# Differential attention: coefficients once per head, scores one step ahead of their maxima, combination and products later

## The chip, the cores and the metric

The kernel runs on one core of one Trainium2 chip. The metric is the device time of one execution in microseconds (us). TensorE is called PE below (its weight loads PEld), VectorE DVE, ScalarE ACT, GpSimd POOL, and SyncE, which issues most of the weight loads from memory, SP.

## What is computed

One inference step of a four-layer trunk on 384 tokens: 128 context tokens and 256 latent ones. The layers mix tokens by differential attention, windowed attention, axial attention and a recurrent scan, in this order, and each is followed by a gated feed-forward. The change is in layer 0, the differential attention: each of 8 heads has two score maps, and the output uses the difference of their softmaxes.

```python
def block(qb, _):
    s = jnp.einsum('bqhmd,bkhmd->bhmqk', qb, keys) * (HEAD_DIM ** -0.5)
    p = jax.nn.softmax(s, axis=-1)
    a = p[:, :, 0] - lam * p[:, :, 1]
    return jnp.einsum('bhqk,bkhe->bqhe', a, vals)
```

Latent queries see 128 cached context keys and 256 latent keys (384 columns); context queries see 128 keys. After the block the head's output is normalised and goes through the output matrix.

## The kernel before

**Layout.** Weights stream in 512 KB units (SP), are split into a rounded and a remainder part (ACT `w_hi`, DVE `w_lo`), and each product is done three times over these parts (`mm3`, lines 394 to 397). Beside this, rows of the conditioning matrices ("ada" units, 512 KB each, issued by POOL into three buffers) are turned into modulation columns. Such a unit has one of two forms (`ada_parts`, line 311): on PE it is a `product` of 16 small matmuls (L336), an ACT copy `row` (L339), and a `turn` of two matmuls (L345) with a DVE copy (L346); on DVE it is two long multiply-reduce instructions (`reduce`, L327).

**Layer 0's attention** (`attn_layer`, line 762) is 24 items `i = (c, t)`: 8 heads `c`, and for each head the query chunks `t` in the order 1, 2, 0, two with 384 keys and then the one with 128. The work of an item is cut into functions: `scores` (two maps on PE, one PSUM bank each, lines 962 to 980), `maxima` (DVE, one per map), `exps` (ACT, one per map, each with its row sum), `inverse` and `coefficient` (DVE, one column each), `combine` (DVE, first map plus coefficient times second), `turn_p` (PE transposes, ACT copy), `pv` (PE products with the values). At a head's end come `finish` (ACT squares), `finish_2` (a chain of small DVE and ACT steps and one DVE multiply), and `turn_o` (PE transposes, ACT `oh` and DVE `ol`, L1107 to L1115).

**Order.** A list of events (lines 1134 to 1166) places every function in a step by a number and within the step by a rank: `at(e, rank, f)`. `advance()` plays one step in order of rank. Step 0 is played inside the last projection slice, steps 1 to 24 in a loop (line 1252) in which PE and DVE run exactly in the written order. ACT and SP run in written order in the whole kernel. So each engine's queue is this list, and an instruction that waits holds back all that stands behind it on its engine. The steps that are left after 24 are handed to `w_o` (line 653), the output matrix, which plays one or more after each of its first rounds `k`. There the planner may interleave PE's and DVE's instructions.

In step `e` the list before is: scores of item e (rank 0); an ada unit in some steps (`fill`, rank 0.5 in the steps with e mod 6 = 0, 1, 4; at rank 1.6 for e mod 6 = 2, 5; here the units of steps 0, 1, 4 mod 6 are in the PE form, the others one DVE reduce each); inverse of item e-1 (1.0); first maximum of item e (1.1); coefficient of e-1 (1.2); second maximum of e (1.3); combine of e-1 (1.5); exps of e (3); turn_p of e-2 (4); turn_o of an earlier head (4.5); pv of e-3 (5); `fill_end`, the turn of the ada unit (5.5); finish of a head (6).

**Buffers.** Scores use four PSUM banks in rotation (`banks(s=(0, 1, 2, 4), ...)`, line 1186), two per item, so the scores of item e take the banks of item e-2 and need its maxima and exps done. The same ring gives the first four blocks of `w_o` their banks. Transposes, ada products and ada turns share two banks (`tr`). The probabilities `p` have seven buffers, the statistics `ast` three.

Of the kernel before, what the change touches and what calls it, by code (L numbers as in the profile page):

```python
# [9 lines left out]
F32 = mybir.dt.float32  # L10
# [3 lines left out]
ALU = mybir.AluOpType  # L14
# [5 lines left out]
TOK = 384  # L20
# [35 lines left out]
RS = (0,1,2,4)  # L56
N7 = 4
PREP = 3
RK = (1.0, 1.1, 1.2, 1.3, 1.5, 2.5, 5.5)
DBANKS = dict(acc=(4, 5, 1, 2, 3), tr=(7, 0, 6))  # L60
RMS_AT = 1
ATT_A = (2, 3, 1, 1, 2, 1, 0)
ATT_B = (3, 4, 2, 1, 1, 3, 0)
LN_EXP = "natural_log_exp_and_others"
SILU = "silu_and_others"
# [83 lines left out]
def trunk(ctx: ExitStack, tc: tile.TileContext, a):  # L149
    nc = tc.nc  # L150
    V, S, G, T = nc.vector, nc.scalar, nc.gpsimd, nc.tensor
# [5 lines left out]
    sm = ctx.enter_context(tc.tile_pool(name="sm", bufs=4))  # L157
# [19 lines left out]
    def work(n=TOK):  # L177
        return wk.tile([128, n], F32, name="w", tag="w")
# [36 lines left out]
    st = dict(dma=0, split=0, blk=0, col=0, raw={}, hi={}, lo={}, look=3)  # L215
# [546 lines left out]
    def attn_layer(li, att, nd):  # L762
        diff = li == 0
# [8 lines left out]
        if diff:  # L772
            lamv = att.tile([128, 4, 64], F32, name="lamv", tag="lamv")
            lam = att.tile([128, 4], F32, name="lam", tag="lam")
            neglam = lam[:, 3:4]
# [174 lines left out]
        events, state, out, last = {}, {}, {}, [None]  # L950

        def at(e, rank, f, *args):
            events.setdefault(e, []).append((rank, len(events.get(e, [])), f, args))
# [2 lines left out]

        def stats_of(c):
            if ("st", c) not in state:
                state["st", c] = sm.tile([128, 8, 6], F32, name="ast", tag="ast", bufs=3)
            return state["st", c]  # L960

        def scores(i, c, t):
# [19 lines left out]
        def maxima(m, i, c, t):  # L982
            j, ps = 2 * t + m, state["s", i][m]
            V.tensor_reduce(out=stats_of(c)[:, 0, j:j + 1], in_=ps, op=ALU.max, axis=AX.X, negate=True)  # L984

        def exps(i, c, t):
            st_ = stats_of(c)
            state["p", i] = []
            for m, ps in enumerate(state.pop(("s", i))):
                j = 2 * t + m  # L990
                w = ps.shape[1]
                p = att.tile([128, TOK + 1], F32, name="p", tag="p")
                S.activation(out=p[:, :w], in_=ps, func=AF.Exp, bias=st_[:, 0, j:j + 1], accum_out=st_[:, 1, j:j + 1])  # L993
                state["p", i].append(p[:, :w - (li == 1)])

        def inverse(i, c, t):
            j = slice(2 * t + int(diff), 2 * t + 2)
            V.reciprocal(out=stats_of(c)[:, 2, j], in_=stats_of(c)[:, 1, j])

        def coefficient(i, c, t):  # L1000
            st_ = stats_of(c)
            V.scalar_tensor_tensor(out=st_[:, 2, 2 * t:2 * t + 1], in0=st_[:, 1, 2 * t:2 * t + 1], scalar=neglam,
                                   in1=st_[:, 2, 2 * t + 1:2 * t + 2], op0=ALU.mult, op1=ALU.mult)

        def combine(i, c, t):

# [127 lines left out]
        n_items = len(items)  # L1134
        tl, pl, cl, man, pend_at, n0, r0 = ATT_A if diff else ATT_B
        for i, (c, t) in enumerate(items):
            args = (i, c, t)
            at(i, 0, scores, *args)
            if diff:
                at(i + 1, RK[0], inverse, *args)  # L1140
                at(i, RK[1], maxima, 0, *args)
                at(i + 1, RK[2], coefficient, *args)
                at(i, RK[3], maxima, 1, *args)
                at(i + 1, RK[4], combine, *args)
                at(i, 3, exps, *args)
                for rank, what in ADA_A[i % len(ADA_A)]:
                    at(i, rank, fill, what)
                at(i + int(RK[6] < 0), abs(RK[6]), fill_end)
            else:
                at(i + 1, 1, maxima, 0, *args)  # L1150
                at(i + 1, 1.1, maxima, 1, *args)
                at(i + 1, 3, exps, *args)
                at(i + cl, 3.1, inverse, *args)
                for m in range(2):
                    at(i + cl, 3.2, divide, m, *args)
            at(i + tl, r0 + 4, turn_p, *args)
            at(i + pl, r0 + 5, pv, *args)
            if i % 3 == 2:
                at(i + pl, r0 + 6, finish, c)
                if not diff:  # L1160
                    at(i + pl + 1, 3.3, finish_low, c)
                if diff:
                    f = i + pl
                    for step_, (e, r) in enumerate(FIN):
                        at(f + e, r, finish_2, step_, c)
                    at(f + FIN[-1][0] + 1, r0 + 4.5, turn_o, c)
        place = [0]

        def advance():
            e = place[0]  # L1170
            place[0] += 1
            for _, _, f, args in sorted(events.pop(e, []), key=lambda x: x[:2]):
                f(*args)
            return e
# [76 lines left out]
        with tc.manual_schedule(engines={mybir.EngineType.PE, mybir.EngineType.DVE}) if man else nullcontext():  # L1251
            while place[0] < n_items + 1:
                i = advance()
# [292 lines left out]
    def body():  # L1546
        nd = None
        for li in range(4):
            ad["limit"] = (LIM0, 144, 184, 184)[li]
            if li == 3:  # L1550
                while ad["done"] < ad["load"]:
                    ada_step()
                ada_ctx.close()
            with ExitStack() as es:
                pool = es.enter_context(tc.tile_pool(name=f"mix{li}", bufs=1))
                nd = attn_layer(li, Att(pool), nd) if li < 3 else hgrn_layer(li, pool, nd)
            banks(acc=(2, 3, 4, 5, 0, 1) if li < 3 else (5, 1, 0, 2, 3, 4), tr=(6, 7))
            ad["limit"] = min((li + 2) * 48 - LIMF, ad["load"]) if li < 3 else 192
            st["look"] = LOOKF[li]
            with ExitStack() as es:  # L1560
                if li == 3:
                    more_ada(es.enter_context(tc.tile_pool(name="ada3", bufs=1)))
                nd = ffn(li, nd, es.enter_context(tc.tile_pool(name=f"ffn{li}", bufs=1)))

    class Att:
        BUFS = dict(xh=3, p=7)

        def __init__(self, pool):
            self.pool = pool
# [1 line left out]
        def tile(self, shape, dt, name, tag, bufs=None):  # L1571
            return self.pool.tile(shape, dt, name=name, tag=tag, bufs=bufs or self.BUFS.get(tag, 1))

# [118 lines left out]
```

## Time and profile before

| what | value |
|---|---|
| median of 3 runs | 1898.87 us (1896.47 to 1899.49) |
| the profiled execution, its own time | 1898.86 us |
| its span in the profile | 1897.1 us |
| granted PE clock, mean | 0.996 of full speed |
| busy share of the span | PE 99%, DVE 80%, ACT 47%, POOL 6% |
| attention steps of layer 0 | from about 125 us to about 187 us of the span |

The span is what the profiler saw of the program; the execution's own time is 1.8 us longer. A busy share says how long an engine had an instruction in work, not that the instruction was needed then. In a row of the timeline the first number is the start from the span's start, the second the time taken, then engine, line, operation, output and inputs; in brackets stands how long the engine had been idle before, and what it had waited for. [...]

### The profile page before, as it was taken

Reading aid. Unit: us, or ns where it says so; the run is one execution under the profiler, and the core shown is the slowest. Engines: PE = TensorE matmul, PEld = TensorE weight load, DVE = VectorE, ACT = ScalarE, POOL = GpSimd, SP = SyncE. Lnnn points to the kernel's source line nnn. Section 1 sums busy time; section 2 is a strip of 40 time slices with the busy share of each in tenths; the row PEclk is TensorE's granted clock in tenths of the full one; section 3 lists DMA queues with packets and bytes.
Section 4 is the critical chain, followed back from the end, with each engine's and each line's share of the span. In section 5 each row is a group of like instructions: output and inputs, shape, how many; then the busy total and the mean of one; then the engine's idle time right before and its main releaser. Section 6 shows DMA issues by size and latency. Waiting matters only on the chain.

```text
span 1897.1 us, 29939 instructions
## 1 busy us (share of the span) xinstructions
PE 1871.4 (99%) x11200; PEld 1744.5 (92%) x11200; DVE 1523.2 (80%) x3012; ACT 896.2 (47%) x1754; POOL 109.1 (6%) x207
## 2 busy tenths in 40 slices
PE   9998999999999999999999999999999999999999
PEld 6876999999975999999975999999989989999999
DVE  6999899995788999994688999994758897964442
ACT  6458553234467553234467553234456665632331
POOL 0011001110000001110000001110000000000000
PEclk9999999999999999999999999999999999999999
DMA  9664568775330558774330568774433324554442
GB/s 373 221 190 140 156 195 264 253 260 161 111 117 1 175 186 263 255 258 141 109 117 1 172 187 265 253 240 132 122 112 113 110 89 140 169 166 129 121 127 67
DMA packets 90741, 315.93 MB, mean 167 GB/s; under 512 B 10976, under 2 KB 14944, under 8 KB 90340
## 3 DMA queue, kind: packets, MB, share of 16 engines
q1 hardware_dynamic: 63508, 217.86, 36.0%
q0 software_dynamic: 26656, 95.97, 16.3%
q8 instruction: 88, 1.44, 0.3%
q14 instruction: 57, 0.47, 0.1%
q10 hardware_dynamic: 432, 0.20, 0.0%
HBM read 309.78 MB, written 4.20 MB: 166 GB/s over the span
## 4 chain that ended last, share of the span: by engine, by line
PE 91%; DVE 5%; ACT 3%; DMA 1%; issue 0%; ACTq 0%; DVEq 0%; SPq 0%
PE b L395 24%; PE b L397 24%; PE b L396 24%; PE b L628 3%; PE b L629 3%; PE b L632 3%; PE b L514 2%; PE b L970 1%; ACT p L993 1%; PE b L1064 1%; PE b L1040 1%; DVE ast L984 1%; PE b L911 1%; DMA ada<-in_ada_dram 0%; DVE junk L327 0%
## 5 line engine op out<-in xcount | busy, mean ns | idle before, releaser
L243 DVE TENSOR_TENSOR wl<-raw,wh 128x1024 fp32r<-128x1024 f32 x384 | 467.2, 1221 | 156.0 <-ACT wh L233 155.5
L233 ACT CAST wh<-raw 128x1024 fp32r<-128x1024 f32 x384 | 399.1, 1047 | 352.5 <-PE b L396 198.0
L397 PE MATMUL b<-fhh,wl 128*128 128x384 f32 x1280 | 433.9, 339 | 0.0
L396 PE MATMUL b<-fhl,wh 128*128 128x384 f32 x1280 | 432.4, 338 | 0.0
L395 PE MATMUL b<-fhh,wh 128*128 128x384 f32 x1280 | 432.4, 338 | 0.0
L327 DVE CUSTOM_DVE_ANT_0 junk<-ada,condb 128x1024 bf16<-128x1024 f32 x312 | 380.1, 1218 | 2.2
L397 PEld LDWEIGHTS b<-fhh,wl 128*128 128x128 f32 x1280 | 241.8, 189 | 0.0
L396 PEld LDWEIGHTS b<-fhl,wh 128*128 128x128 f32 x1280 | 241.8, 189 | 0.0
L395 PEld LDWEIGHTS b<-fhh,wh 128*128 128x128 f32 x1280 | 241.5, 189 | 0.0
L395 PE MATMUL b<-fh,wh 128*128 128x384 f32 x704 | 239.0, 339 | 0.0
L397 PE MATMUL b<-fh,wl 128*128 128x384 f32 x704 | 237.4, 337 | 0.0
L396 PE MATMUL b<-fl,wh 128*128 128x384 f32 x704 | 237.4, 337 | 0.0
L699 ACT CAST fh<-w 128x384 fp32r<-128x384 f32 x88 | 45.2, 514 | 288.2 <-DVE w L705 280.2
L395 PE MATMUL b<-xh,wh 128*128 128x386 f32 (+1 forms) x448 | 155.1, 346 | 0.0
L397 PE MATMUL b<-xh,wl 128*128 128x386 f32 (+1 forms) x448 | 152.6, 341 | 0.0
L396 PE MATMUL b<-xl,wh 128*128 128x386 f32 (+1 forms) x448 | 151.5, 338 | 0.0
L298 POOL DMA_DIRECT2D ada<-in_ada_dram x176 | 93.3, 530 | 986.8 <-DVE mod L327 771.4
L397 PEld LDWEIGHTS b<-fh,wl 128*128 128x128 f32 x704 | 132.3, 188 | 0.0
L396 PEld LDWEIGHTS b<-fl,wh 128*128 128x128 f32 x704 | 132.2, 188 | 0.0
L395 PEld LDWEIGHTS b<-fh,wh 128*128 128x128 f32 x704 | 132.1, 188 | 0.0
L412 DVE SCALAR_TENSOR_TENSOR x<-b,mod,x 128x128 f32<-128x128 f32 x192 | 69.6, 411 | 40.0 <-PE b L397 39.8
L705 DVE TENSOR_TENSOR w<-b,w 128x384 f32<-128x384 f32 x80 | 44.4, 555 | 58.8 <-PE b L397 58.6
(263 smaller groups left out, 2856.0 us busy)
## 6 DMA issues: line engine op xcount, KB each, us to landing
raw<-in_w_dram SPq DMA_DIRECT2D x384, 512.0 KB, 4.3
ada<-in_ada_dram POOLq DMA_DIRECT2D x176, 512.0 KB, 4.6
a0s<-in_ada_dram SPq DMA_DIRECT2D x8, 512.0 KB, 9.6
ada<-in_ada_dram SPq DMA_DIRECT2D x8, 512.0 KB, 9.6
x<-in_x_dram SPq DMA_DIRECT2D x4, 384.0 KB, 5.3
out_y_dram<-x SPq DMA_DIRECT2D x8, 192.0 KB, 1.9
condb<-saved SPq DMA_DIRECT2D x1, 1024.0 KB, 11.7
s<-in_state_dram POOLq DMA_DIRECT2D x8, 128.0 KB, 2.4
```

What stands on the lines that cost most here:

```text
L233: S.copy(out=hi, in_=st["raw"][u])
L243: V.tensor_tensor(out=lo, in0=st["raw"].pop(u), in1=st["hi"][u].bitcast(F32), op=ALU.subtract)
L298: (nc.gpsimd if i >= 16 else nc.sync).dma_start(out=t, in_=a["ada"][i])
L327: V.tensor_tensor_reduce(out=ad["junk"], in0=raw, in1=ad["cond"][:, j, :], op0=ALU.mult, op1=ALU.add, scale=1.0, scalar=0.0, accum_out=out ...
L395: T.matmul(out=out, lhsT=lh, rhs=rh, start=start, stop=False)
L396: T.matmul(out=out, lhsT=lh, rhs=rl, start=False, stop=False)
L397: T.matmul(out=out, lhsT=ll, rhs=rh, start=False, stop=stop)
L412: V.scalar_tensor_tensor(out=x[:, d, c0:c1], in0=ps[:, c0:c1], scalar=gate[:, d, j:j + 1], in1=x[:, d, c0:c1], op0=ALU.mult, op1=ALU.add)
L628: T.matmul(out=ps[t], lhsT=hh[:, k, c], rhs=wh, start=k == 0, stop=False)
L629: T.matmul(out=ps[t], lhsT=hh[:, k, c], rhs=wl, start=False, stop=False)
L632: T.matmul(out=ps[t], lhsT=hl[:, k, c], rhs=wh, start=False, stop=k == KC - 1)
L699: S.copy(out=fh[:, j, :], in_=m)
```

## The change

It moves the places in the list. The scores of item e stay in step e, and its maxima and exps come in step e+1. The two column operations that were done for each item (`inverse`, `coefficient`) are done once for a head over three columns (`coefficients`, at rank 1.0 in the step after the head's last exps). Combine comes four steps after the item's scores (`cl`, before one), `turn_p` five (before two), `pv` six (before three). The turn of an ada unit (`fill_end`) moves from rank 5.5 of its own step to rank 0.4 of the next one, behind that step's scores. To hold more items in flight, the statistics get five buffers, the first map's probabilities six, and the second map's go into the ring of five work tiles. `inverse` itself remains for the other layers.

```diff
--- before.py
+++ after.py
@@ -56,10 +56,10 @@
 RS = (0,1,2,4)
 N7 = 4
 PREP = 3
-RK = (1.0, 1.1, 1.2, 1.3, 1.5, 2.5, 5.5)
+RK = (1.0, 1.1, 1.2, 1.3, 1.5, 2.5, -0.4)
 DBANKS = dict(acc=(4, 5, 1, 2, 3), tr=(7, 0, 6))
 RMS_AT = 1
-ATT_A = (2, 3, 1, 1, 2, 1, 0)
+ATT_A = (5, 6, 4, 1, 2, 1, 0)
 ATT_B = (3, 4, 2, 1, 1, 3, 0)
 LN_EXP = "natural_log_exp_and_others"
 SILU = "silu_and_others"
@@ -956,7 +956,7 @@
 
         def stats_of(c):
             if ("st", c) not in state:
-                state["st", c] = sm.tile([128, 8, 6], F32, name="ast", tag="ast", bufs=3)
+                state["st", c] = att.tile([128, 8, 6], F32, name="ast", tag="ast", bufs=5 if diff else 3)
             return state["st", c]
 
         def scores(i, c, t):
@@ -989,18 +989,20 @@
             for m, ps in enumerate(state.pop(("s", i))):
                 j = 2 * t + m
                 w = ps.shape[1]
-                p = att.tile([128, TOK + 1], F32, name="p", tag="p")
+                p = work(TOK) if diff and m else att.tile([128, TOK + 1], F32, name="p", tag="p", bufs=6 if diff else 7)
                 S.activation(out=p[:, :w], in_=ps, func=AF.Exp, bias=st_[:, 0, j:j + 1], accum_out=st_[:, 1, j:j + 1])
                 state["p", i].append(p[:, :w - (li == 1)])
 
         def inverse(i, c, t):
-            j = slice(2 * t + int(diff), 2 * t + 2)
+            j = slice(2 * t, 2 * t + 2)
             V.reciprocal(out=stats_of(c)[:, 2, j], in_=stats_of(c)[:, 1, j])
 
-        def coefficient(i, c, t):
+        def coefficients(c):
+
             st_ = stats_of(c)
-            V.scalar_tensor_tensor(out=st_[:, 2, 2 * t:2 * t + 1], in0=st_[:, 1, 2 * t:2 * t + 1], scalar=neglam,
-                                   in1=st_[:, 2, 2 * t + 1:2 * t + 2], op0=ALU.mult, op1=ALU.mult)
+            V.reciprocal(out=st_[:, 2, 1:6:2], in_=st_[:, 1, 1:6:2])
+            V.scalar_tensor_tensor(out=st_[:, 2, 0:6:2], in0=st_[:, 1, 0:6:2], scalar=neglam,
+                                   in1=st_[:, 2, 1:6:2], op0=ALU.mult, op1=ALU.mult)
 
         def combine(i, c, t):
 
@@ -1137,12 +1139,12 @@
             args = (i, c, t)
             at(i, 0, scores, *args)
             if diff:
-                at(i + 1, RK[0], inverse, *args)
-                at(i, RK[1], maxima, 0, *args)
-                at(i + 1, RK[2], coefficient, *args)
-                at(i, RK[3], maxima, 1, *args)
-                at(i + 1, RK[4], combine, *args)
-                at(i, 3, exps, *args)
+                at(i + 1, RK[1], maxima, 0, *args)
+                if i % 3 == 2:
+                    at(i + 2, 1.0, coefficients, c)
+                at(i + 1, RK[3], maxima, 1, *args)
+                at(i + cl, RK[4], combine, *args)
+                at(i + 1, 3, exps, *args)
                 for rank, what in ADA_A[i % len(ADA_A)]:
                     at(i, rank, fill, what)
                 at(i + int(RK[6] < 0), abs(RK[6]), fill_end)
@@ -1563,7 +1565,7 @@
                 nd = ffn(li, nd, es.enter_context(tc.tile_pool(name=f"ffn{li}", bufs=1)))
 
     class Att:
-        BUFS = dict(xh=3, p=7)
+        BUFS = dict(xh=3)
 
         def __init__(self, pool):
             self.pool = pool
```

## Rows read from the trace of the kernel before

**Rows 1.** Busy time of each engine in stretches: the attention loop, the output matrix

```profile
core 0: us, PE busy (x) PEld busy (x) DVE busy (x) ACT busy (x) POOL busy (x), PEclk, DMA share, GB/s
...
140.00:155.00 15.00, 13.05 (x128) 9.35 (x129) 13.87 (x52) 12.60 (x54) 2.39 (x5) 1.00 0.43 142
...
200.00:212.00 12.00, 12.00 (x69) 11.49 (x68) 10.27 (x25) 6.35 (x15) 0.00 (x0) 1.00 0.42 132
```

**Rows 2.** Waits between 125 and 194 us: engine, line, releaser, total us, times, longest

```profile
DVE ast L998 <- ACT p L993: 2.9, 9, 0.5
...
ACT p L993 <- DVE ast L984: 8.6, 17, 1.3
```

**Rows 3.** Timeline of DVE, 161 to 168 us, steps 13 to 16

```profile
161.65 0.56 DVE L984 TENSOR_REDUCE ast<-b 128x1 f32<-128x384 f32 x1 [0.25 <-PE b L970]
...
163.93 0.15 DVE L346 COPY mod<-b 128x2 f32<-128x2 f32 x1
...
164.18 0.27 DVE L984 TENSOR_REDUCE ast<-b 128x1 f32<-128x128 f32 x1
...
164.70 0.61 DVE L1008 SCALAR_TENSOR_TENSOR p<-p,ast 128x384 f32<-128x384 f32 x1
165.23 1.22 DVE L327 CUSTOM_DVE_ANT_0 junk<-ada,condb 128x1024 bf16<-128x1024 f32 x1
...
166.37 0.61 DVE L1114 SCALAR_TENSOR_TENSOR ol<-b,subg,oh 128x384 fp32r<-128x384 f32 x1
166.90 0.15 DVE L998 RECIPROCAL ast<-ast 128x1 f32<-128x1 f32 x1
166.97 0.54 DVE L984 TENSOR_REDUCE ast<-b 128x1 f32<-128x384 f32 x1
167.43 0.21 DVE L1002 SCALAR_TENSOR_TENSOR ast<-ast,lam 128x1 f32<-128x1 f32 x1
```

**Rows 4.** Timeline of PE, 160 to 164 us, steps 13 and 14

```profile
160.70 0.92 PE L970 MATMUL b<-kT,qT 64*128 64x384 f32 x4
161.96 0.64 PE L336 MATMUL b<-ada,condP 128*32 128x128 f32 x16 [0.34 <-ACT pt L1023]
...
163.37 0.28 PE L345 MATMUL b<-quarter,row 128*128 128x2 f32 x2
163.58 0.49 PE L970 MATMUL b<-kT,qT 64*128 64x128 f32 x4
```

**Rows 5.** Timeline of ACT, 159 to 175 us, steps 12 to 18

```profile
159.94 0.58 ACT L993 ACTIVATE p<-b,ast 128x384 f32<-128x384 f32 x1 [0.87 <-DVE ast L984]
...
161.01 0.19 ACT L993 ACTIVATION_READ_ACCUMULATOR p<-b,ast 128x1 f32 x1
...
162.83 0.59 ACT L993 ACTIVATE p<-b,ast 128x384 f32<-128x384 f32 x1
...
171.62 0.37 ACT L993 ACTIVATE p<-b,ast 128x128 f32<-128x128 f32 x1 [0.56 <-DVE ast L984]
...
172.23 0.20 ACT L993 ACTIVATION_READ_ACCUMULATOR p<-b,ast 128x1 f32 x1
...
172.69 0.60 ACT L1113 ACTIVATE oh<-b,subg 128x384 fp32r<-128x384 f32 x1
...
174.68 0.58 ACT L993 ACTIVATE p<-b,ast 128x384 f32<-128x384 f32 x1 [0.46 <-DVE ast L984]
```

**Rows 6.** Timeline of all engines: exps of items 1 and 22, first w_o product

```profile
135.22 0.21 ACT L993 ACTIVATION_READ_ACCUMULATOR p<-b,ast 128x1 f32 x1
...
185.45 0.19 ACT L993 ACTIVATION_READ_ACCUMULATOR p<-b,ast 128x1 f32 x1
...
185.77 0.44 PE L395 MATMUL b<-oh,wh 128*128 128x384 f32 x1
```

**Rows 7.** Chain of waits near the loop's end: start, us, what

```profile
184.63 0.67 PE b L1052 x6
...
186.56 0.33 PE b L1021 x3
```

## The prediction

> **What bounds the kernel now.** I read the windows first, to see what the changed stage is short of. In the attention loop DVE is busy 13.87 of 15 us, PE 13.05, ACT 12.60; in the output matrix after it PE is busy the whole time [rows 1]. So a microsecond of PE work costs its full price behind the loop and little inside it, where DVE is nearly full. Then the waits: over the loop DVE loses only 2.9 us, to the exps that its reciprocal needs, and ACT loses 8.6 us, waiting for a maximum [rows 2]. Then the timeline, for the pace. From the exps of step 12 to those of step 18 it takes 174.68 - 159.94 = 14.74 us for six steps, two heads [rows 5].
>
> The round that sets this pace is: exps end, DVE's reciprocal, first maximum, next exps. DVE fills the gaps with combine, reduces and the heads' ends. PE is ahead of this round: the scores of step e need the banks of item e-2, whose exps ended a step earlier.
>
> **The prices.** A pair of exps takes 161.01 + 0.19 - 159.94 = 1.26 us with 384 keys, and 172.23 + 0.20 - 171.62 = 0.81 with 128 [rows 5]. A first maximum takes 0.54 (128 keys: 0.27), and the next DVE instruction starts 0.46 behind its start; combine 0.53, reduce 1.14 and the head's `ol` 0.53 from start to start [rows 3]. Both score maps take 0.92 (128 keys: 0.49), a turn 0.28 [rows 4]. That the first maximum waits for both maps is seen in its start at 161.65, 0.95 after the scores' [rows 3, 4]. From a product's start to the exps behind its row copy it is 162.83 - 161.96 = 0.87 [rows 4, 5]. From a 128-key pair's end to the end of `oh` it is 172.69 + 0.60 - 172.43 = 0.86 [rows 5].
>
> **Part by part.** *Coefficients once per head.* Of 24 reciprocals and 24 coefficients 8 each are left. The next instruction starts 0.07 behind a reciprocal, and a coefficient takes at most its 0.21 [rows 3]; 32 fewer give 16 × 0.07 + 16 × 0.21 = 4.5 us at most. DVE also no longer waits for each exps, up to the 2.9 us [rows 2]. This counts only where DVE sets the end.
>
> *Scores one step ahead.* Now the exps of item e-2 run in step e-1, so the scores of step e, the first thing on PE in that step, wait for the exps just ended. Everything behind them on PE waits too: the turn, the product, transposes and pv. The four banks are the limit, and the change adds none.
>
> *The turn moved behind the scores.* Its DVE copy is now the first DVE instruction of the step, ahead of coefficients, maxima and combine. In steps 1, 2 and 5 of six a turn is pending, so DVE stands until exps end, scores, turn, copy (0.15 [rows 3]), and only then forms the maximum that the next exps need. From exps end to exps end:
> - Steps 2 and 5 (the new scores are 128 keys): 0.49 + 0.28 + 0.15 + 0.54 + 1.26 = 2.72.
> - Step 1 (384 keys, coefficients first, reciprocal 0.15 and coefficient 0.21 in sequence): 0.92 + 0.28 + 0.15 + 0.36 + 0.54 + 1.26 = 3.51.
> - Step 4 has no turn but a product, whose ACT copy stands ahead of the exps: 0.92 + 0.87 + 1.26 = 3.05.
> - Steps 2 and 3 together go by DVE: copy ends at 0.92, two maxima 0.92, combine 0.53, reduce 1.14, which is 3.51. `ol` waits for `oh` until 2.72 + 0.86 = 3.58; with it 4.11, the 128-key maximum 0.27, the pair 0.81: 5.19.
> - Steps 5 and 0 together: the product's path is longer, 2.72 + 0.92 + 0.87 + 0.81 = 5.32.
>
> Six steps are 3.51 + 5.19 + 3.05 + 5.32 = 17.07 us, against 14.74.
>
> *Start and end of the loop.* Before, the exps of item 1 end at 135.43 and those of item 22 at 185.64, 21 steps in 50.21 us [rows 6]. After, item 0's exps fall in step 1, at about the place of item 1's (taken as equal), and item 22's in step 23, 22 steps later: three sixes, 51.21, and steps 20 to 23, 2.72 + 2.47 + 3.05 + 2.72 = 10.96. The first steps lack work: step 2 has no combine and no `ol` yet (1.13 less for steps 2 and 3), step 8 no `ol` (0.6 less). That makes 60.4 us, 10.2 more. The first product of the output matrix takes the bank of item 22's first map and starts at 185.77, 0.13 after those exps [rows 6], so this delay reaches PE's next work whole.
>
> *Work moved past the loop.* Combine, transposes and products of three more items and one more head's end fall into the output matrix. On PE: 7 transposes at 0.11, 7 products of two instructions at 0.11 each, 3 transposes of the head: 10 × 0.11 + 14 × 0.11 = 2.6 us [rows 7]. Much of it runs while PE waits for the last exps; bounds 0 and 2.6, I take 0.8, since two of the three items' work stands in the waiting steps 23 and 24. On DVE it is 1.6 us of combines beside 10.27 busy of 12 [rows 1]; cover: DVE's free 14%, and 1.6 us if that is gone.
>
> *Edits at nothing.* More buffers: the item that had a buffer before is combined or turned a step before it is asked for. The second map's ring has no other user inside the loop; cover gone, exps would wait one combine, 0.5. The ada units' POOL loads are issued when a product has been copied out, now a turn later; three buffers cover 0.28. SP issues nothing inside the loop, and its weight loads move with the loop.
>
> **Sum**: 10.2 + 0.8 = 11.0 us. The profiled execution, 1898.86 us, is the median of the runs to 0.01, so 1909.9, rounded to **1910**. Bounds: the second map alone, its partner started earlier, could need 0.67 (six of 0.11 [rows 7] as the nearest row of that length) in place of 0.92, and the 128-key one 0.33 in place of 0.49. Per six steps that is at most 2 × 0.25 + 2 × 0.16 = 0.8, in all 3 us less. Upward the moved PE work adds 1.8 and uncounted semaphore time of 0.1 in 22 steps 2.2. The case by itself: 1906 to 1914.
>
> *A switch of shape on PE.* Scores use halves of the array (64 rows), the ada product 32 columns, the turn the full array. The turn now stands between scores and product, one more change of shape in each of 12 steps. In the trace the scores at 163.58 start 0.21 after the turn, before its 0.28 have passed [rows 4]: I take nothing for it. [...]
>
> **Rivals.** *A. DVE is the only limit, and the change gives.* It holds if scores and turn are always done before DVE reaches the copy, that is, if DVE is more than 0.49 + 0.28 (or 0.92 + 0.28) us behind the exps in the turn steps. For it: 13.87 of 15 us on DVE [rows 1]. Against it: DVE waits for the exps already now [rows 2], and sheds work. Its price: the 2.9 of waits and some 2.6 of the 4.5 (half of the coefficients' time overlaps), and 2.6 less DVE work in the loop (three combines, one head's end, less item 0's maxima) are gained, the 2.6 of PE work behind the loop is paid, -5.5 net: 1893.4.
>
> *B. The gate is there but half as long*, since scores of the first map start early and maxima, row copy and turn overlap better than I add them: half of 11 us, 1904; from there it fades to no change at 1899.
>
> *C. The tail hurts more.* The last head's `turn_o` is played after round 6 of the output matrix, before after round 4, just ahead of round 7 that needs it. Against it: later blocks can be worked on meanwhile. Price up to two rounds' slack of 12 instructions of 12.00 / 69 = 0.17 each [rows 1], 4 us on top of the forecast: 1914 and more.
>
> **Numbers.** Forecast 0.60, A 0.17, B 0.18, C 0.05. The likeliest gives 1910. The range goes from 1897 to 1914: down over B and its fading, leaving out A's full gain and half of C. About 0.2%, 3.8 us, is what a measurement of this kernel can tell from no change. Faster takes A, 0.16; within 0.2% takes the rest of A and two thirds of B, 0.13; slower the rest, 0.71.
>
> **What would show it.** Right: in the changed kernel DVE's copy L346 stands with idle time before it, released by PE's turn L345, in half of the steps; scores L970 wait for exps L993; six steps take about 17 us; DVE is busy under 13 of 15 us in the loop, and the output matrix starts near 196 us. Wrong: no wait ahead of L346, six steps under 14.7, or the loop's end at or before 185.8. If the loop is as slow as said and the whole is not, the step on the moved work is wrong.

## The result and the profile after

| | before | after |
|---|---|---|
| median, runs of one comparison | 1897.67 us (4 runs) | 1915.19 us (4 runs, 1914.42 to 1915.91) |
| ratio, 95% interval | 1 | 1.0091 [1.0079, 1.0103] |
| profiled execution, span | 1898.86, 1897.1 us | 1915.58, 1913.8 us |
| granted PE clock, mean | 0.996 | 0.992 |

The change makes the kernel 17.5 us slower by the medians and 16.7 by the two profiled executions. All medians here are of fast runs: single executions far above the others, one each of e3 and e8 and one of the kernel before, are left out. The forecast was 1910, the range 1897 to 1914: the direction was right, the loss was larger than the range allowed for.

The windows over the loop of the changed kernel (columns as in [rows 1]):

```profile
core 0: us, PE busy (x) PEld busy (x) DVE busy (x) ACT busy (x) POOL busy (x), PEclk, DMA share, GB/s
124.00:140.00 16.00, 13.22 (x86) 9.24 (x85) 9.98 (x23) 7.45 (x19) 2.14 (x4) 0.86 0.57 183
140.00:155.00 15.00, 12.74 (x90) 7.82 (x87) 6.84 (x20) 5.74 (x24) 2.12 (x4) 0.70 0.33 106
155.00:170.00 15.00, 13.15 (x88) 8.60 (x89) 10.65 (x34) 9.58 (x42) 1.42 (x3) 0.89 0.24 71
170.00:185.00 15.00, 13.51 (x105) 9.23 (x103) 11.20 (x38) 9.60 (x41) 1.21 (x3) 1.00 0.45 141
```

DVE, 13.87 of 15 us busy before [rows 1], has 6.84 to 11.20 left, and ACT 5.74 to 9.60 of its 12.60. PE's busy time stays near its 13.05, but with 88 to 105 instructions in place of 128. The column to look at is the granted clock. It was 1.00 from 140 to 155 us before; now it is 0.70 there, and 1.00 only from 170 us on. The waits from 125 to 215 us (columns as in [rows 2]) name the chain:

```profile
DVE mod L346 <- PE b L345: 23.5, 12, 4.8
...
ACT row L339 <- PE b L336: 16.6, 10, 2.8
ACT p L993 <- DVE ast L984: 12.7, 10, 2.1
...
PE b L970 <- ACT p L993: 7.7, 12, 1.4
```

PE waits for the exps, DVE's copy L346 for PE's turn, ACT for DVE's maximum: the three sides of the forecast's gated step. L346 stands 12 times in 24 steps, for 23.5 us, the longest wait of DVE, ACT or PE (POOL, which issues the ada loads, stands longer for its buffers, 34.2 us for L1023 alone, as it did before, 31.7 for L336). Two steps at full clock, in the timeline of all engines from 170 us (steps 13 and 14):

```profile
170.42 0.20 ACT L993 ACTIVATION_READ_ACCUMULATOR w<-b,ast 128x1 f32 x1
...
170.78 0.92 PE L970 MATMUL b<-kT,qT 64*128 64x384 f32 x4
...
171.63 0.38 PE L345 MATMUL b<-quarter,row 128*128 128x2 f32 x2
171.94 0.64 PE L336 MATMUL b<-ada,condP 128*32 128x128 f32 x16
172.05 0.16 DVE L346 COPY mod<-b 128x2 f32<-128x2 f32 x1 [1.67 <-PE b L345]
...
172.68 0.83 PE L1054 MATMUL b<-vt,pt 128*128 128x128 f32 x6
...
173.05 0.58 ACT L993 ACTIVATE p<-b,ast 128x384 f32<-128x384 f32 x1
...
173.20 0.55 DVE L984 TENSOR_REDUCE ast<-b 128x1 f32<-128x384 f32 x1
...
173.78 0.48 PE L970 MATMUL b<-kT,qT 64*128 64x128 f32 x2 [0.26 <-ACT p L993]
...
174.26 0.19 ACT L993 ACTIVATION_READ_ACCUMULATOR w<-b,ast 128x1 f32 x1
...
174.51 0.48 PE L970 MATMUL b<-kT,qT 64*128 64x128 f32 x2 [0.25 <-ACT w L993]
...
175.34 0.16 DVE L346 COPY mod<-b 128x2 f32<-128x2 f32 x1 [0.53 <-PE b L345]
...
176.73 1.47 PE L970 MATMUL b<-kT,qT 64*128 64x384 f32 x4 [0.40 <-ACT p L993]
```

Exps end at 170.62, scores start 0.16 later, then turn, copy, maximum and the next exps, whose pair ends at 174.45: step 13 took 3.83 us against a forecast of 3.51. In step 14 the two score maps start apart, each when its own bank's exps end, 0.48 each, where before both took 0.49 together [rows 4].

The clock in short stretches. First after:

```profile
132.00:136.00 4.00, 2.64 (x26) 1.56 (x25) 1.09 (x3) 2.73 (x8) 1.08 (x2) 0.92 0.75 223
136.00:140.00 4.00, 2.58 (x8) 1.91 (x8) 2.63 (x7) 1.51 (x6) 0.00 (x0) 0.50 0.35 131
...
146.00:152.00 6.00, 5.40 (x31) 3.62 (x31) 2.64 (x7) 2.82 (x11) 1.05 (x2) 0.50 0.33 117
...
160.00:162.00 2.00, 2.00 (x9) 1.71 (x10) 1.71 (x10) 1.10 (x5) 0.00 (x0) 0.50 0.02 4
```

The first of them before:

```profile
132.00:136.00 4.00, 3.52 (x34) 1.93 (x34) 3.51 (x10) 3.48 (x10) 1.08 (x2) 1.00 0.76 173
136.00:140.00 4.00, 3.26 (x33) 1.73 (x29) 3.46 (x11) 2.65 (x11) 0.24 (x1) 1.00 0.67 268
```

In the first steps PE has little to do, since transposes and products now come five and six steps behind the scores, and it stands waiting besides: busy 2.64 of 4 us, before 3.52. The granted clock then falls to 0.50 (136 to 142 us), the lowest value in any window read here. How the gated step looks at 0.50 (146 to 152 us), in PE's timeline from 144 us (step 6):

```profile
146.60 2.21 PE L970 MATMUL b<-kT,qT 64*128 64x384 f32 x4 [1.03 <-ACT p L993]
148.74 1.08 PE L336 MATMUL b<-ada,condP 128*32 128x128 f32 x16
...
150.45 1.49 PE L1054 MATMUL b<-vt,pt 128*128 128x128 f32 x6
```

The 2.21 holds a wait as well, since the second map starts only when its own bank's exps end. Scores gated in the same way take 1.47 at full clock (176.73), the products of the ada unit 0.64 and those with the values 0.83 (171.94, 172.68). The copy of step 7, whose turn stands behind all this, waited 4.8 us, the longest of its 12 waits.

The last exps and the first product of the output matrix, in the timeline of all engines from 202 us, answer to [rows 6]:

```profile
202.53 0.44 PE L395 MATMUL b<-oh,wh 128*128 128x384 f32 x1 [0.40 <-ACT p L993]
...
202.84 0.20 ACT L993 ACTIVATION_READ_ACCUMULATOR w<-b,ast 128x1 f32 x1
```

Item 22's exps end 203.04 - 185.64 = 17.4 us later, the output matrix starts 202.53 - 185.77 = 16.8 later, and the span is 16.7 longer. The whole loss lies ahead of the output matrix.

### The profile page after: what moved, and what is told of

Same layout as the page of the kernel before. It is cut to its first block, busy times and chain, and to the rows that moved or that the text cites. A ratio compares the mean times of both kernels' runs of the same rounds, so it can differ in the third digit from the quotient of the medians.

```text
span 1913.8 us, 29898 instructions
## 1 busy us (share of the span) xinstructions
PE 1887.0 (99%) x11200; PEld 1754.1 (92%) x11200; DVE 1521.5 (80%) x2980; ACT 896.5 (47%) x1754; POOL 108.9 (6%) x207
## 4 chain that ended last, share of the span: by engine, by line
PE 91%; DVE 5%; ACT 3%; DMA 1%; issue 0%; ACTq 0%; DVEq 0%; SPq 0%
PE b L395 24%; PE b L397 24%; PE b L396 24%; PE b L628 3%; PE b L629 3%; PE b L632 3%; PE b L970 2%; PE b L514 2%; PE b L1066 1%; PE b L1042 1%; DVE ast L984 1%; ACT p L993 1%; PE b L911 1%; DMA ada<-in_ada_dram 0%; PE b L1054 0%
## 5 line engine op out<-in xcount | busy, mean ns | idle before, releaser
L395 PE MATMUL b<-fhh,wh 128*128 128x384 f32 x1280 | 431.9, 337 | 0.0
L395 PEld LDWEIGHTS b<-fhh,wh 128*128 128x128 f32 x1280 | 240.3, 188 | 0.0
L395 PE MATMUL b<-fh,wh 128*128 128x384 f32 x704 | 237.8, 338 | 0.0
L395 PE MATMUL b<-xh,wh 128*128 128x386 f32 (+1 forms) x448 | 155.1, 346 | 0.0
L395 PEld LDWEIGHTS b<-fh,wh 128*128 128x128 f32 x704 | 132.2, 188 | 0.0
```

What stands on the lines that cost most here:

```text
L395: T.matmul(out=out, lhsT=lh, rhs=rh, start=start, stop=False)
```

## The experiments

Ratios are to the kernel before on the same chip, with the 95% interval. "Output matrix" is the start of its first product L395: 185.77 before, 202.53 after.

### Where the turn stands

**e1_turn_own_step**: the changed kernel with the turn back in its own step.

```diff
-RK = (1.0, 1.1, 1.2, 1.3, 1.5, 2.5, -0.4)
+RK = (1.0, 1.1, 1.2, 1.3, 1.5, 2.5, 5.5)
```

> The changed kernel with one thing put back: the turn of an ada unit stands at the end of its own step (rank 5.5) and no longer behind the next step's scores. Theory G (the scores wait for the exps just ended, and the DVE copy behind the turn hands that wait to DVE): DVE's copy L346 no longer waits (23.5 us in the changed kernel, under 4 here), the product's row copy still stands behind gated scores in steps 0, 1, 4 of six, so six steps take about 14 to 15 us in place of 17.5, and the time is 1901 to 1908. Rival D (the loss comes from the deeper pipeline: work moved past the loop, longer rings): 1913 to 1916, as the changed kernel.

1898.84 us, 1.0006 [0.9997, 1.0016]: the loss is gone, and more of it than expected, although the copy still waits 7.3 us where under 4 was expected. Its wait for the turn, and the exps six steps apart (ACT's timeline, steps 13 and 19):

```profile
DVE mod L346 <- PE b L345: 7.3, 6, 2.9
```

```profile
162.80 0.59 ACT L993 ACTIVATE p<-b,ast 128x384 f32<-128x384 f32 x1
...
177.40 0.59 ACT L993 ACTIVATE p<-b,ast 128x384 f32<-128x384 f32 x1
```

Six steps take 14.60 us, against 14.74 before. Scores issued ahead do little harm by themselves: the interval ends 3 us above before. The turn behind them does the rest.

**e3_turn_alone**: the other half, the kernel before with the turn moved and nothing else (the same line, 5.5 to -0.4, in the kernel before).

> The kernel before with only the turn moved behind the next step's scores (rank 0.4 of the next step). Theory G: there the scores need banks that came free a step earlier, so nothing of the wait is handed on; 1896 to 1901. Rival S (the moved turn costs by itself: a change of shape on PE more in 12 steps, a DVE copy ahead of the maxima): 1903 or more.

1899.90 us, 1.0005 [0.9995, 1.0014]. The turn behind the scores does little harm either, as long as the scores don't wait for exps: in the profiled execution six steps take 15.17 us (step 12 to step 18), 0.43 more than before, and the interval's upper end is 2.7 us. Only the two together cost 17.5. The run also has the further change of shape on PE, 12 times.

**e10_scores_behind_turn**: the changed kernel, with the scores moved behind turn and ada product.

```diff
-            at(i, 0, scores, *args)
+            at(i, 0.6 if diff else 0, scores, *args)
```

> The changed kernel with the scores at rank 0.6, behind the pending turn and the product of their step and ahead of transposes and pv; the turn stays in the next step (rank 0.4). Theory G: turn and product no longer stand behind scores that wait for exps, so neither DVE's copy nor ACT's row copy inherits the wait; DVE's copy waits under 5 us in all (23.5 in the changed kernel), six steps in 13.3 to 14.6 us, 1893 to 1899. If the turn's place in the next step were itself the cost: 1910 or more.

1903.54 us, 1.0029 [1.0020, 1.0039]. The exps of steps 13 and 19 in ACT's timeline, and the windows from 140 to 148 us:

```profile
164.50 0.59 ACT L993 ACTIVATE p<-b,ast 128x384 f32<-128x384 f32 x1
...
179.39 0.58 ACT L993 ACTIVATE p<-b,ast 128x384 f32<-128x384 f32 x1
```

```profile
140.00:144.00 4.00, 4.00 (x25) 2.09 (x17) 2.91 (x8) 2.08 (x8) 0.53 (x1) 0.50 0.41 124
144.00:148.00 4.00, 4.00 (x27) 2.39 (x27) 2.08 (x6) 2.35 (x9) 1.05 (x2) 0.50 0.25 71
```

Six steps take 14.89, so in the full loop the order alone gives the pace back (14.74 before), a little short of the 13.3 to 14.6 expected. The copy waits 10.4 us in 8 places, where under 5 was expected, and the output matrix starts at 189.53. What is left goes mostly with the clock, which the expectation had left out: it is 0.50 from 140 to 148 us, and of the ten runs the three with a mean granted clock of 0.997 take 1899.4 to 1900.0 us, the seven with 0.992 to 0.994 take 1902.5 to 1906.8.

### The clock

**e5_filler**: the changed kernel with four products of ones into bank 5 at the end of steps 1 to 8; nothing reads them. **e9_filler_off_path**: the same in steps 1 to 5 and 8 only. **e8_turn_own_filler**: e1 with the filler of e5.

```diff
+            for e in range(1, 9):
+                at(e, 5.1, warm, 4)
```

> The changed kernel with four PE products of ones at the end of each of steps 1 to 8, into a bank nothing reads (about the work of the transposes and pv that these steps do not have yet). Theory K (in the first steps PE has so little to do that the granted clock falls to its lower level, and gated PE work then takes twice as long): granted clock 1.00 in all of 132 to 165 us, where the changed kernel shows 0.50 to 0.94, and 5 to 7 us less, 1908 to 1911. Without K (the slow first steps have another cause): 1915 or more.

> The changed kernel with the filler of four products of ones (0.9 us of PE) only at the end of steps 1 to 5 and 8, where the changed kernel's PE stood idle about 1 us before the next scores; steps 6 and 7, where the filler delayed the scores, are left as they are. Theory K: granted clock near 1.00 up to 160 us and 4 to 7 us less than the changed kernel, 1908 to 1911. Without K: 1914 or more, whatever the clock shows.

> The changed kernel with the turn at the end of its own step (1898.8 alone) and the filler of four products of ones at the end of steps 1 to 8. Theory K: that run showed a granted clock of 0.50 to 0.87 between 142 and 148 us; with the filler 1.00 there and 1 to 2.5 us less, 1896 to 1898. If the filler's own PE time is on the path, 1899 to 1902.

e5: 1912.84, 1.0081 [1.0065, 1.0097]. e9: 1911.74, 1.0073 [1.0057, 1.0088]. e8: 1901.42, 1.0018 [1.0009, 1.0027]. The windows of e9, and the ends of the exps of steps 1, 7 and 13, first in the changed kernel and then in e9 (ACT's timeline):

```profile
132.00:136.00 4.00, 3.58 (x34) 2.44 (x34) 1.09 (x3) 2.60 (x8) 1.08 (x2) 1.00 0.76 220
136.00:140.00 4.00, 3.58 (x21) 2.45 (x21) 2.70 (x8) 2.04 (x8) 0.00 (x0) 1.00 0.33 118
...
172.00:176.00 4.00, 3.99 (x13) 2.64 (x13) 3.67 (x13) 3.63 (x17) 0.00 (x0) 0.57 0.00 0
```

```profile
135.65 0.21 ACT L993 ACTIVATION_READ_ACCUMULATOR w<-b,ast 128x1 f32 x1
...
155.44 0.20 ACT L993 ACTIVATION_READ_ACCUMULATOR w<-b,ast 128x1 f32 x1
...
174.26 0.19 ACT L993 ACTIVATION_READ_ACCUMULATOR w<-b,ast 128x1 f32 x1
```

```profile
135.53 0.21 ACT L993 ACTIVATION_READ_ACCUMULATOR w<-b,ast 128x1 f32 x1
...
152.28 0.20 ACT L993 ACTIVATION_READ_ACCUMULATOR w<-b,ast 128x1 f32 x1
...
169.55 0.19 ACT L993 ACTIVATION_READ_ACCUMULATOR w<-b,ast 128x1 f32 x1
```

With useless work on PE the clock holds at 1.00 to 172 us, and the kernel is faster for it: 3.5 us by the medians, 3.4 by the two ratios. The intervals overlap a little, but each of its four runs is faster than each of the changed kernel's four; 1908 to 1911 was expected. From the exps of step 1 to those of step 7 it takes 16.74 us (19.78 in the changed kernel), from step 7 to step 13 17.26 (18.81): 4.6 us less. Of this 1.0 goes again in a fall of the clock at 172 to 176 us (18.52 us for the next six steps, 17.49 in the changed kernel). L346 still waits 19.9 us and the loss is still 13.6: the clock made the loss larger, it is not its cause. e5 holds the clock at 1.00 to 172 us as well and gains less than expected: with filler in steps 6 and 7 too, the exps of step 7 end 4.38 us behind those of step 6, in e9 3.55. The "twice as long" of its expectation is 1.7 and 1.8 times in the changed kernel's rows at 0.50 (1.08 against 0.64, 1.49 against 0.83). In e8, where PE waits only 0.3 us from 125 to 194, it is busy 15.00 of 15 us from 140 to 155 at a clock of 1.00, and step 1 to step 7 takes 15.04 us, in e1 14.22: the filler costs there more than it saves.

### Where the scores stand

**e2_scores_last**: scores at the end of the step (rank 5.2 in place of 0), turn as changed. **e7_scores_last_turn_own**: this with e1's turn.

> The changed kernel with the scores of a step issued last on PE in that step (rank 5.2), behind turn, product, transposes and pv; maxima and exps still one step later. Theory G: nothing but the scores waits for the exps any more; DVE sets the pace, six steps in 13.3 to 14.5 us, time 1894 to 1903. Rival D: 1912 or more, since depth, rings and moved work are those of the changed kernel.

> The changed kernel with the scores last on PE in their step and the turn at the end of its own step (rank 5.5, behind these scores). Theory G: as the run with scores last (1904.2) or up to 6 us less, since no ACT-gated transposes stand ahead of the turn's copy: 1896 to 1904. If the time stays at 1904 the loss of that run lies elsewhere, in the transposes that wait for their bank ahead of the scores.

1904.18, 1.0036 [1.0021, 1.0050], and 1902.77, 1.0026 [1.0015, 1.0038]. Most of the loss goes, but less than with e1. The waits of e2 show what stands ahead of the scores now:

```profile
DVE mod L346 <- PE b L345: 10.2, 9, 3.4
...
PE b L1023 <- ACT pt L1025: 2.7, 5, 0.9
```

Transposes, ada products and turns share two banks, and wait for ACT's copy out of them; ACT copies behind the exps. So a wait for the exps comes back by another bank; this is read from the waits, and no run tried it alone.

### Without the lead of the scores

**e6_same_step_turn_own**: maxima and exps back in the scores' own step, coefficients a step earlier, turn as before; coefficients once per head and the late combine stay.

```diff
-                at(i + 1, RK[1], maxima, 0, *args)
+                at(i, RK[1], maxima, 0, *args)
...
-                    at(i + 2, 1.0, coefficients, c)
-                at(i + 1, RK[3], maxima, 1, *args)
+                    at(i + 1, 1.0, coefficients, c)
+                at(i, RK[3], maxima, 1, *args)
...
-                at(i + 1, 3, exps, *args)
+                at(i, 3, exps, *args)
```

**e4_not_ahead**: the same with the turn as changed and every distance one less, `ATT_A = (4, 5, 3, ...)`. **e11_same_step_filler**: e6 with 2, 2 and 3 products of ones at the ends of steps 2, 3 and 4. **e12_same_step_filler_nearer**: e11 with `ATT_A = (4, 6, 3, ...)`.

> The changed kernel with maxima and exps back in the scores' own step; coefficients once per head, combine, turn_p and pv keep their distance to the exps (3, 4 and 5 steps), the turn stays behind the next step's scores. Theory G: the scores' banks are free a step before, so the copy finds its turn done; six steps 14 to 14.8 us, 1894 to 1901, plus up to 3 us if the granted clock dips in the first steps, where PE has no transposes or products yet. Rival D: 1908 or more.

> The changed kernel with maxima and exps back in the scores' own step and the turn at the end of its own step; what is left of the change is coefficients once per head, and combine, turn_p and pv four to six steps behind the scores. Theory G: no gate on scores or turn, DVE spared the per-item columns and its waits for exps: 13.3 to 14.6 us for six steps, 1893 to 1899. Rival D (depth and the work moved past the loop cost): 1902 or more. The run with maxima and exps back but the turn left behind the scores and all distances one shorter gave 1904.8.

> The run with maxima and exps in the scores' own step and the turn at its old place ended the loop 2.8 us earlier than before, although its granted clock fell to 0.57 at 140 to 144 us. Added here: 2, 2 and 3 products of ones at the ends of steps 2, 3 and 4, where PE stands. Theory (the clock falls because PE has too little to do in the thin first steps): the clock stays at 1.00 at 140 to 144, the ada product and the transposes there take 0.65 and 0.55 again instead of 1.08 and 0.90, the loop ends 1 to 2 us earlier still (first output-matrix product at 181 to 182), and the time is 1896 to 1897.5. Rival (the fall has another cause, or the filler costs as much on PE's path as it saves): the output matrix starts at 183 or later, 1897.5 to 1899.

> As the run beside it, with combine three steps behind the scores in place of four and the transposes four in place of five (products six, as changed), which is the nearest that one coefficient step per head allows. Theory (the 2.6 us of PE work moved past the loop costs time there): three transposes and a combine less lie behind the loop, 0.3 us of PE, so the time is that of its neighbour or up to 0.5 us less. Rival (the reciprocal of a head now stands ahead of a combine that needs it in the same step and waits for the exps just ended): DVE's reciprocal waits in 8 steps, 0.3 each, and the time is 1 to 3 us above its neighbour.

e4: 1904.82, 1.0038 [1.0024, 1.0051], a miss. DVE's `ol` waits 8.8 us in 8 places for ACT's `oh` there, 2.2 in two heads, and six steps take 16.9 us, 2.2 more than before. That products five steps behind the scores bring this about, by moving each head's end one step against the ada units, is argued and not shown. L346 waits 5.0 us in 6 places, as in e3 (4.8 in 6), so the moved turn is not what is new; the run says nothing on the lead.

e6: 1897.74, 0.9998 [0.9989, 1.0007]; e11: 1898.24, 0.9998 [0.9989, 1.0007]; e12: 1896.80, 0.9990 [0.9981, 0.9999]. In e6 the output matrix starts at 182.96, 2.8 us earlier than before, in e11 at 183.59, in e12 at 182.56. From there to the end of the span they take 1712.0, 1713.1 and 1713.7 us, where before and the changed kernel both take 1711.3: 0.7 to 2.4 us are given back behind the loop. The moved PE work (its bound was 2.6) does not explain it: the changed kernel, and e1 with 1709.8, move as much of it as e6 and e11 and give nothing back, and e12, which moves less, gives back most. Single executions of the kernel before differ by as much, from 1896.30 to 1900.12, and the granted clock falls behind the loop too, not always by the same (it is 0.89 before from 1000 to 1030 us, and 0.94 in the changed kernel from 1016.8 to 1046.8). What takes the gain stays open. In e6 the clock falls in the loop as well:

```profile
136.00:140.00 4.00, 2.75 (x31) 1.58 (x29) 3.74 (x11) 3.20 (x13) 0.53 (x1) 1.00 0.77 262
140.00:144.00 4.00, 4.00 (x31) 3.21 (x31) 2.83 (x9) 2.39 (x9) 1.05 (x2) 0.57 0.40 100
```

In e11:

```profile
136.00:140.00 4.00, 4.00 (x39) 2.58 (x40) 3.88 (x10) 2.66 (x12) 0.53 (x1) 1.00 0.68 274
140.00:144.00 4.00, 4.00 (x42) 2.71 (x42) 3.71 (x11) 2.53 (x11) 1.05 (x2) 1.00 0.47 133
```

The clock is held, but from item 1's exps to item 22's only 0.6 us is gained (47.67 against 48.24), and no time; 1 to 2 us were expected. DVE is busy 3.88 and 3.71 of 4 us in these two windows, so it has little room left. e12 is the only kernel of the study whose interval lies below 1, by 1.6 us and barely; that is less than the 0.2% taken as the bound. Its rival, a reciprocal that waits for the exps, did not appear: DVE stands nowhere ahead of L1003 in the list of waits.

## Why the prediction was right in kind and wrong in size

**The gate and the turn: right, and shown.** The waits that it named are there, L346 for the turn with 23.5 us, L970 for the exps with 7.7. e1 and e3 show that neither the lead nor the moved turn alone costs more than 3 us of the 17.5, and e10 that the order of turn and scores brings back the pace. That the four score banks make the gate is read from the waits; more banks were not tried, since the other four (3, 5, 6, 7) hold products and transposes.

**The steady pace: right within 0.4.** Step 13 to step 19 takes 17.49 us, step 17 to 23 takes 17.48, against 17.07. Most of the missing part is in step 13, 3.83 for 3.51: 0.16 from exps to scores, 0.07 more from there to the copy, and a pair of exps of 1.40 in place of 1.26, since its second exps waits for a maximum that ends at 173.75. The forecast had time between instructions in its upper bound, not in its sum; the 0.1 a step there was an estimate that no row was named for, and the 0.16 is what was measured from exps to scores.

**The first steps: wrong, and this is the step that failed.** The prediction wrote that "the first steps lack work" and took 1.13 and 0.6 off for them. It asked only which instructions are missing there, not what PE does meanwhile. From the end of the exps of step 1 to those of step 7 it was 19.78 where 17.07 - 1.13 was forecast, to step 13 another 18.81 for 17.07 - 0.6: 3.84 and 2.34 more, 6.2 in all. By e9, 4.6 of that goes with the granted clock; the rest is the steady pace's shortfall of 0.42 twice over and 0.8 that the filler doesn't mend. With the clock held to 172 us the kernel takes 1911.74, which is inside the range. The account to the end of item 22's exps: 10.2 forecast, 0.43 from a later start, 3.84, 2.34, 0.42 in the third six and 0.14 in the last four steps, together 17.4. No term for the clock stood in the sum, nor in a rival or in the range, because the profile before showed 1.00 in the whole loop; so the range was too short upward.

The granted clock in the windows is 1.00, 0.50 or between them. The first fall comes within a stretch in which PE is busy 0.99 of 2 us (134 to 136, clock 0.84). Not every such stretch brings a fall: before, PE is busy 1.05 of 2 us at 158 to 160, and the clock stays at 1.00. By what rule it falls is not shown; e5 and e9 show that with more work on PE it stays at 1.00 to 172 us.

**Moved work behind the loop: too high.** 0.8 was taken; the output matrix starts 16.8 later and the span is 16.7 longer, so nothing is seen of it, and nothing in e1, e9 and e10 (1709.8, 1711.4 and 1711.2 us from there to the end). That this work stands in PE's waits is argued. The 0.7 to 2.4 us of e6, e11 and e12 do not go with it, as said there.

**Rival A** (DVE alone decides, 1893): refuted by the waits ahead of L346. **Rival B** (half the gate, 1904): refuted at full clock too, since e9 still loses 13.6. **Rival C** (the tail): not seen, by the same 16.8 and 16.7. **The switch of shape**: taken at nothing; e3's 0.43 in six steps would allow 0.14 for each of three turns. A whole turn for each of the 12, 12 × 0.28 = 3.4 us, would have put e3 3.4 us above before; its interval ends at 2.7. In e3 a turn behind scores takes 0.38 us (PE's timeline, 162.81) where it took 0.28 behind products [rows 4]; no run shows a change of shape by itself.

**The rest of the change.** Coefficients once per head and a late combine are worth no more than e6 and e12 show, 0 to 1.6 us: six steps take 14.76 us in e6, so what DVE is spared does not show in the pace.

## What to carry to other kernels

An instruction that is moved behind a gated one on its engine carries that gate to whoever waits for it: here PE's turn took the wait for exps to DVE's first instruction (L346, 23.5 us), and closed a circle over three engines, though each of the two moves alone cost 3 us at most. Before scores are issued a step ahead, count whose banks they take and when those come free. And when work is pushed later in a pipeline, look at what PE has left in the first steps: a stretch where it waits can cost twice, by the wait and by the clock that it is granted afterwards. Here PE was busy 2.64 of 4 us, the clock then fell to 0.50, and filler that held it at 1.00 to 172 us gave back 3.5 us of the 17.5.

## What was not expected of the hardware

A kernel became faster with products that nobody reads: e9 keeps the clock at 1.00 to 172 us and gains 3.5 us. Nearly the same filler made e8, which waits less, slower than e1 by 2.6. And a fall of the clock in one stretch need not show in the whole: e1 shows 0.87 and 0.70 in the windows 140 to 144 and 144 to 148 us, and its output matrix starts 1.5 us later. In its profiled execution the stretch behind is 1.5 us shorter than before, which no run here explains, and its median is that of before.
